# A reordered DeltaNet preparation in a hybrid encoder layer

## The chip, the cores and the metric

The kernel runs on one core of one Trainium2 chip. A core has a matrix engine (TensorE, in the profile PE, with its weight loads as PEld), a vector engine (VectorE, DVE), a scalar engine (ScalarE, ACT), a general engine (GpSimd, POOL) and a queue engine (SyncE, SP) that here issues nearly all transfers. The metric is the device time of one execution in microseconds (us); lower is better.

## The reference, cut to what matters

One encoder layer is applied with the same weights to two sequences, 1024 and 256 tokens of width 1024. The kernel treats them as ten tiles of 128 tokens.

```
h = RMSNorm_pre(x);  p = h @ w_in            # 3088 columns
group A: bidirectional gated DeltaNet, 4 heads of 128
    q, k, v = silu(depthwise conv of 5 taps (p columns))
    q, k normalised to unit length; per head a decay g and a gain beta, per direction
    in chunks: tri = I + strict_lower(beta * k k^T * decay); solve tri against (beta v, beta k exp(cum g))
    a state of 128x128 is carried from chunk to chunk
    o = o_forward + o_backward;  o = RMSNorm(o) * silu(z)
group B: bidirectional attention, 4 query heads, 2 key heads, RMS-normalised q and k, 2-D rotary positions
x = x + RMSNorm(concat(o_A, o_B) @ w_out)
x = x + RMSNorm(relu(RMSNorm(x) @ w_up)^2 @ w_down)
```

All arithmetic that matters is kept to about 32 bits: a factor is split into a high part and a low part (`split`, lines 79 and 80), and a product is three matmuls.

## The kernel before, in words

The kernel is one function, `build`, traced from top to bottom. A planner then fixes the order of the instructions on each engine: what is traced earlier has the higher priority, and a later instruction is put ahead only where the planner expects the earlier one not to be ready. Each engine, and each DMA queue, then works strictly in the fixed order and waits where an input or a buffer is not ready. A buffer is named by a tag with a number of copies; a tile that takes a copy waits until the last reader of the tile before it is done.

The layer goes through these stages:

1. *Normalisation and z* (0 to 96 us). `x_proc` (lines 176 to 185) normalises a token tile (square on ACT, an inverse root in ten small DVE steps, a multiplication on DVE), transposes it on PE and splits it into `h_hi` and `h_lo`. `load_block` loads and splits the weights of the z columns; the low parts are subtracted on POOL (`leng=G`). `nat_z` multiplies, ten tiles in turn. Masks (`incl`, `strict`, `identr`, `nmask`, lines 237 to 246) are traced after that loop, but nothing keeps the planner from putting them first.
2. *Preparation* (96 to 525 us), the loop over `ORDER` at the end of the first half. Its parts are generators, and each word of `ORDER` runs one of them as far as its next `yield`:
   - `K` (`gdn_qk`): for a head, projects k, then its convolution (`conv_proj`), transposes k (L459), writes decayed keys; the same for q (transposes L473); then the inverse lengths.
   - `V` (`gdn_v`): the same for v (transposes L502).
   - `E` (`gdn_e`), five parts of two tiles: decay exponents `pe` by matmuls (L516, L522) with a right side `ER` (L518: one direction on POOL, one on DVE), `E = exp(pe)` (L523), products `pk` of k with k and q (L528), and from both the tiles `A` (L529) and `C` (L531).
   - `S` (`gdn_sub`): inverts the 32x32 diagonal blocks of C, with a chain of 62 DVE instructions per head (L560, L561).
   - `L` (`gdn_lev`): two levels that build the inverse of 128x128 from these blocks, with small matmuls (L589 to L625).
   - `a` (`att_proj`): an attention column block; j = 0 to 3 are queries, 4 and 5 keys, 6 and 7 values. Projects, transposes on PE for the sums of squares (L400), and for queries and keys applies the rotary positions: the rows swapped in groups of 32 are got by writing the block to DRAM (`aqkv_d`, L391) and loading it back swapped (`axw`, L394). Keys are multiplied by a broadcast inverse length, `prk` (L423, L426).
   Every projection (`proj_T`, L367 to L369) is 72 matmuls. They need `h_hi` and `h_lo`, whose space the attention stage takes over afterwards.
3. *Attention with the DeltaNet scan* (525 to about 800 us): the first scores (L712) need the keys and queries loaded from DRAM (`load_rot`, L663); the scan loads what the preparation wrote to `vis_d` (`vis_load`, L652).
4. *Output projection and the feed-forward part*, to the end.

PSUM has eight banks: in the preparation `mm` has three (projections), `tr` two (`pe` and `pk` among others), and `tq` (kt, qt, vt), `iv` (levels) and `at` (attention transposes, `prk`) one each.

Of the kernel before, what the change touches and what calls it, by code (L numbers as in the profile page):

```python
# [38 lines left out]
ORDER = (  # L39
    "K0 K0 K0 K0 E0 E0 E0 E0 K1 E0 K1 S0 K1 K1 L0 E1 E1 V0 V0 E1 E1 L0 E1 K2 K2 K2 K2 E2 E2 E2 V1 E2 E2 "  # L40
    "V1 S1 K3 S2 K3 K3 L1 L1 V2 K3 L2 V2 V3 V3 E3 L2 a0 a0 E3 E3 a4 E3 E3 a4 S3 L3 a5 L3 a5 a6 a6 a1 a1 "
    "a2 a2 a3 a3 a7 a7"
)
# [18 lines left out]
def build(ctx, tc, I, O):  # L62
# [48 lines left out]
    z_d = dr.tile([TOK, 512], F32, name="z_d")  # L111
    aqkv_d = [dr.tile([128, TOK], F32, name=f"aqkv{j}_d") for j in range(6)]
    arot_d = [dr.tile([128, TOK], F32, name=f"arot{j}_d") for j in range(8)]
# [14 lines left out]
    tr_tile = b_tile("tr", 2, ps)  # L128
    tq_tile = b_tile("tq", 1)
    iv_tile = b_tile("iv", 1)  # L130
    at_tile = b_tile("at", 1)
    ch_tile = b_tile("ch", 2)
# [44 lines left out]
    def x_proc(t, x):  # L177
        junk = xs.tile([128, DM], F32, tag="junk", name="junk", bufs=1)
        ss = xs.tile([128, 1], F32, tag="ss", name="ss", bufs=3)
        S.activation(junk, x, AF.Square, accum_out=ss)  # L180
        rs = xs.tile([128, 1], F32, tag="rs", name="rs", bufs=3)
        rsqrt(xs, rs, ss, 1, 1.0 / DM, "n0")
        xn = xs.tile([128, DM], F32, tag="xn", name="xn", bufs=2)
        V.scalar_tensor_tensor(xn, x, rs, wpre, ALU.mult, ALU.mult)
        to_T(xs, xn, h_hi, h_lo, t)


    w_in = I["w_in"]

    def load_block(segs):  # L190
        wts = []
        for k in range(KD):
            raw = xp.tile([128, 512], F32, tag="wraw", name="wraw", bufs=4)
            o = 0
            for c0, n in segs:
                SP.dma_start(out=raw[:, o:o + n], in_=w_in[k * 128:(k + 1) * 128, c0:c0 + n])
                o += n
            whi = xp.tile([128, 512], F32R, tag="whi", name="whi", bufs=8)
            wlo = xp.tile([128, 512], F32R, tag="wlo", name="wlo", bufs=8)
            split(whi, wlo, raw, leng=G)  # L200
            wts.append((whi, wlo))
# [21 lines left out]

    x_proc(0, x)
    wz = load_block([(1536, 512)])

# [3 lines left out]
    for t in range(NT):  # L230
        if t + 1 < NT:
            x_proc(t + 1, x_load(t + 1))
        nat_z(t, wz)
# [9 lines left out]
    identr = gc.tile([128, 128], F32R, name="identr")  # L243
    V.tensor_copy(identr, ident)
    nmask = gc.tile([128, 2, 128], F32R, name="nmask")
    V.tensor_scalar(nmask, f32(strict), -1e30, None, ALU.mult)
    ones1 = gc.tile([128, 1], F32, name="ones1")
# [132 lines left out]
    def att_proj(j):  # L380

        if not att:
            rope = gp.tile([128, 2, 1282], F32, tag="qk", name="rope", bufs=2)[:, :, 0:1024]
            SP.dma_start(out=rope, in_=I["c_rope"])
            att[0] = rope
        rope = att[0]
        c = (2064 + j * 128, 2576 + (j - 4) * 128, 2832 + (j - 6) * 128)[max(0, j - 2) // 2]
        raw = tp_.tile([128, TOK], F32, tag="cp", name="araw", bufs=2)
        proj_T(c, raw, ((0, 512, 0), (512, 512, 512), (1024, 256, 1024)))
        if j < 6:  # L390
            SP.dma_start(out=aqkv_d[j], in_=raw)  # L391
            xw = tp_.tile([128, TOK], F32, tag="cy", name="axw", bufs=1)
            for b in range(4):
                SP.dma_start(out=xw[b * 32:b * 32 + 32], in_=aqkv_d[j][(b ^ 1) * 32:(b ^ 1) * 32 + 32])  # L394
        yield
# [12 lines left out]
        if j >= 6:  # L408
            return
        rs = rsa[:, j]  # L410
        rsqrt(gp, rs, ssa[:, j], NT, 1.0 / 128, "na")
# [38 lines left out]
    def gdn_qk(h):  # L450
        qk = gp.tile([128, 2, 1282], F32, tag="qk", name="qk", bufs=2)
        qks[h] = qk
        yield from conv_proj(4 + h, qk[:, 1])
        ssq = gp.tile([128, 2, NT], F32, tag="ssq", name="ssq", bufs=2)
# [12 lines left out]
        yield  # L467
        yield from conv_proj(h, qk[:, 0])
        for t0 in range(0, NT, 4):
# [24 lines left out]
    def gdn_v(h):  # L494
        vT = gp.tile([128, 1282], F32, tag="vT", name="vT", bufs=1)
        yield from conv_proj(8 + h, vT)
        irk = irks[h]
        for t0 in range(0, NT, 4):
# [9 lines left out]
    def gdn_e(h):  # L508
# [3 lines left out]
        for t0, n in ((0, 2), (2, 2), (4, 2), (6, 2), (8, 2)):  # L512
            E = gp.tile([128, 2, 2, 128], F32, tag="E", name="E", bufs=2)
            pe = tr_tile("pe").rearrange("p (d j c) -> p d j c", d=2, j=2)
            for d in range(2):
                T.matmul(pe[:, d], lhsT=identr, rhs=nmask[:, 1 - d:2 - d].to_broadcast([128, 2, 128]), start=True, stop=False)  # L516
                R = gp.tile([128, 2, 2, 128], F32R, tag="ER", name="ER", bufs=1)
                (G if d == 0 else V).tensor_tensor(  # L518
                    R, incl[:, d][:, None, None, :].to_broadcast([128, 2, 2, 128]),
                    f32(gr[:, :, t0:t0 + 2, 4 * d + h])[:, :, :, None].to_broadcast([128, 2, 2, 128]), ALU.mult)  # L520
                for i in range(2):
                    T.matmul(pe[:, d], lhsT=(r_gt, r_lt)[d], rhs=R[:, i], start=False, stop=(i == 1))  # L522
            S.activation(E, pe, AF.Exp)  # L523
            A = gp.tile([128, 2, 2, 128], F32, tag="A", name="A", bufs=1)
            for j in range(n):
                t = t0 + j
                pk = tr_tile("pk")
                T.matmul(pk[:, 0:256], lhsT=qk[:, 1, col(t)], rhs=qk[:, :, col(t)], start=True, stop=True)  # L528
# [10 lines left out]
    def gdn_sub(h):  # L539
        C = Cs[h]  # L540

        Cc = gp.tile([128, 2, NT, 32], F32, tag="Cc", name="Cc", bufs=1)
        for b in range(4):
# [978 lines left out]
```

## Time and profile before

| | |
|---|---|
| time, median of 3 runs | 1723.78 us (1721.43 to 1723.92) |
| time of the profiled execution | 1724.17 us |
| its span in the profile | 1722.4 us |
| busy share of the span: PE, PEld, DVE, ACT, POOL | 94%, 80%, 74%, 49%, 42% |
| mean granted PE clock | 0.985 |
| data moved by DMA | 252.68 MB |

A row of a table of stretches gives the stretch in us from the start of the span, its length, then for each engine the busy time with the number of instructions, the granted PE clock (1.00 is full), the share in which the DMA engines were busy, and GB/s. A row of waits gives the engine, its tile and line, what released it, the total in us, how many times, and the longest. A row of a group of instructions gives line, engine, operation, output and inputs, shape and count; then busy us and the mean of one in ns; then the idle time just before them and what ended it. A row of a timeline gives start, duration, engine, line and operation, and in square brackets the idle time ahead of it with what ended it. A row of DMA issues gives target and source, queue, count, KB of one and the median us from issue to landing. A row for PE shows modelled ends: consecutive matmuls overlap.

### The profile page before, as it was taken

Reading aid. Unit: us, or ns where it says so; the run is one execution under the profiler, and the core shown is the slowest. Engines: PE = TensorE matmul, PEld = TensorE weight load, DVE = VectorE, ACT = ScalarE, POOL = GpSimd, SP = SyncE. Lnnn points to the kernel's source line nnn. Section 1 sums busy time; section 2 is a strip of 40 time slices with the busy share of each in tenths; the row PEclk is TensorE's granted clock in tenths of the full one; section 3 lists DMA queues with packets and bytes.
Section 4 is the critical chain, followed back from the end, with each engine's and each line's share of the span. In section 5 each row is a group of like instructions: output and inputs, shape, how many; then the busy total and the mean of one; then the engine's idle time right before and its main releaser. Section 6 shows DMA issues by size and latency. Waiting matters only on the chain. (4 is left out here: it accounts for less than half of the span.)

```text
span 1722.4 us, 27988 instructions
## 1 busy us (share of the span) xinstructions
PE 1618.9 (94%) x9799; PEld 1383.8 (80%) x9799; DVE 1278.8 (74%) x2562; ACT 851.8 (49%) x1937; POOL 715.4 (42%) x645
## 2 busy tenths in 40 slices
PE   6999898899997999889998999999999999999996
PEld 5877676777776888668877999999998888888885
DVE  7546798997654788885659759555797887887877
ACT  5226567654345767674436546554464333333412
POOL 3212231312113434440103634644335778878852
PEclk9999999999998999999999999999999999999998
DMA  6213344545547866244334445434566444444244
GB/s 201 79 35 105 103 111 127 147 109 164 150 142 222 289 196 206 80 162 157 110 110 132 159 140 177 149 130 141 191 217 214 144 141 143 141 128 146 82 137 150
DMA packets 208779, 252.68 MB, mean 147 GB/s; under 512 B 35073, under 2 KB 163391, under 8 KB 208639
## 3 DMA queue, kind: packets, MB, share of 16 engines
q1 hardware_dynamic: 208495, 250.77, 46.2%
q8 instruction: 77, 1.26, 0.3%
q14 instruction: 63, 0.52, 0.1%
q0 software_dynamic: 144, 0.13, 0.0%
HBM read 159.75 MB, written 91.10 MB: 146 GB/s over the span
## 5 line engine op out<-in xcount | busy, mean ns | idle before, releaser
L1161 PE MATMUL pd<-mh,uhl 128*128 128x320 f32 x892 | 277.5, 311 | 6.0 <-DVE uhl L1152 5.9
L1160 PE MATMUL pd<-mh,uhl 128*128 128x320 f32 x892 | 276.0, 310 | 1.9 <-ACT uhl L1151 1.9
L1162 PE MATMUL pd<-ml,uhl 128*128 128x320 f32 x892 | 276.2, 310 | 0.0
L1309 DVE TENSOR_TENSOR acc<-acc,pd 128x512 f32<-128x512 f32 x330 | 207.4, 679 | 48.4 <-PE pd L1305 47.9
L1303 PE MATMUL pd<-dhi,fhi 128*128 128x512 f32 x490 | 192.2, 392 | 0.9 <-DVE acc L1311 0.9
L1304 PE MATMUL pd<-dl,fhi 128*128 128x512 f32 x490 | 192.3, 392 | 0.0
L1305 PE MATMUL pd<-dhi,flo 128*128 128x512 f32 x490 | 191.9, 392 | 0.0
L367 PE MATMUL pt<-h_hi,whi 128*128 128x512 f32 (+1 forms) x480 | 177.8, 370 | 0.0
L368 PE MATMUL pt<-h_lo,whi 128*128 128x512 f32 (+1 forms) x480 | 177.7, 370 | 0.0
L369 PE MATMUL pt<-h_hi,wlo 128*128 128x512 f32 (+1 forms) x480 | 177.4, 370 | 0.0
L1161 PEld LDWEIGHTS pd<-mh,uhl 128*128 128x128 f32 x892 | 168.3, 189 | 8.6 <-DVE uhl L1152 8.6
L1160 PEld LDWEIGHTS pd<-mh,uhl 128*128 128x128 f32 x892 | 168.0, 189 | 3.6 <-ACT uhl L1151 3.5
L1162 PEld LDWEIGHTS pd<-ml,uhl 128*128 128x128 f32 x892 | 168.1, 188 | 0.0
L1285 ACT CAST fhi<-fr 128x1280 fp32r<-128x1280 f32 x49 | 62.1, 1267 | 201.1 <-PE pd L1304 114.5
L1206 POOL TENSOR_TENSOR s<-u,u 128x320 f32<-128x320 f32 x31 | 28.2, 909 | 252.9 <-ACT u L1170 252.9
L1275 POOL TENSOR_TENSOR dl<-dw,dhi 128x1024 fp32r<-128x1024 f32 x47 | 118.7, 2525 | 28.3 <-ACT dhi L1274 20.8
L1152 DVE TENSOR_TENSOR uhl<-us,uhl 128x512 fp32r<-128x512 f32 x88 | 90.2, 1025 | 37.5 <-ACT uhl L1151 36.6
L727 POOL TENSOR_TENSOR P<-P,sm 128x512 f32<-128x512 f32 (+1 forms) x72 | 73.5, 1042 | 94.9 <-DVE sm L725 40.0
L1303 PEld LDWEIGHTS pd<-dhi,fhi 128*128 128x128 f32 x490 | 92.0, 188 | 22.2 <-issue 1.3
L1305 PEld LDWEIGHTS pd<-dhi,flo 128*128 128x128 f32 x490 | 92.0, 188 | 20.6
L1304 PEld LDWEIGHTS pd<-dl,fhi 128*128 128x128 f32 x490 | 92.0, 188 | 20.5
L1169 ACT ACTIVATE u<-u 128x320 f32<-128x320 f32 x128 | 60.1, 470 | 95.4 <-DVE u L1196 40.8
(369 smaller groups left out, 4116.4 us busy)
## 6 DMA issues: line engine op xcount, KB each, us to landing
fr<-r_d SPq DMA_DIRECT2D x49, 640.0 KB, 3.9
vis<-vis_d SPq DMA_DIRECT2D x64, 384.0 KB, 4.2
uraw<-in_w_up SPq DMA_DIRECT2D x22, 1024.0 KB, 5.4
r_d<-s SPq DMA_DIRECT2D x128, 160.0 KB, 1.8
r_d<-u SPq DMA_DIRECT2D x96, 160.0 KB, 1.9
dw<-in_w_down SPq DMA_DIRECT2D x28, 512.0 KB, 4.3
wraw<-in_w_in SPq DMA_DIRECT2D x48, 256.0 KB, 3.4
x<-in_x_prompt SPq DMA_DIRECT2D x16, 512.0 KB, 3.5
```

The costliest lines, as they stand in the source:

```text
L367: T.matmul(pm[:, :n], lhsT=whi, rhs=h_hi[:, k, t0:t0 + n], start=(k == 0), stop=False)
L368: T.matmul(pm[:, :n], lhsT=whi, rhs=h_lo[:, k, t0:t0 + n], start=False, stop=False)
L369: T.matmul(pm[:, :n], lhsT=wlo, rhs=h_hi[:, k, t0:t0 + n], start=False, stop=(k == KD - 1))
L1152: V.tensor_tensor(lo, ua[n][UP[i][0]], f32(hi), ALU.subtract)
L1160: T.matmul(pm, lhsT=w[0][:, k], rhs=mh[b, i][:, k], start=(k == 0), stop=False)
L1161: T.matmul(pm, lhsT=w[1][:, k], rhs=mh[b, i][:, k], start=False, stop=False)
L1162: T.matmul(pm, lhsT=w[0][:, k], rhs=ml[b, i][:, k], start=False, stop=(k == 3))
L1275: last["pool"] = leng.tensor_tensor(lo, raw, f32(hi), ALU.subtract)
L1303: T.matmul(pm, lhsT=r[0][:, k, tk], rhs=w[0][:, k], start=(k == 0), stop=False)
L1304: T.matmul(pm, lhsT=r[0][:, k, tk], rhs=w[1][:, k], start=False, stop=False)
L1305: T.matmul(pm, lhsT=r[1][:, k, tk], rhs=w[0][:, k], start=False, stop=(k == Q - 1))
L1309: last["dve"] = V.tensor_tensor(half(t, d), half(t, d), pm, ALU.add)
```

## The change

The parts of the preparation are cut differently, listed in another order, and take other buffers.

- `ORDER` is replaced. The sub-block solves S and the E parts of a head come earlier, the attention projections all come after S3, and L3 comes at the very end.
- `gdn_qk`, `gdn_v` and `att_proj` yield once more, so that the transposes of k, q and v come a part after the convolution, and the tail of an attention block a part after its transposes.
- `tq`, `iv` and `at` become one ring of three PSUM banks, `fx`; `pk` moves from `tr` to that ring. `ER` and `A` get a second copy. `Cc` takes the buffer of `Rt`.
- The ER tile of one direction is made by four ACT instructions where POOL made it with one.
- The swapped rows are copied from `raw` to `axw` inside SBUF; `aqkv_d` is gone. `axw` takes the second `qk` buffer and alternates between its two halves.
- The low parts of the z weights are subtracted on DVE, placed behind the first tile's normalisation in DVE's queue (`issue_after` orders instructions of one engine); `identr` and `nmask` are placed behind the normalisation of the last tile.

```diff
 ORDER = (
-    "K0 K0 K0 K0 E0 E0 E0 E0 K1 E0 K1 S0 K1 K1 L0 E1 E1 V0 V0 E1 E1 L0 E1 K2 K2 K2 K2 E2 E2 E2 V1 E2 E2 "
-    "V1 S1 K3 S2 K3 K3 L1 L1 V2 K3 L2 V2 V3 V3 E3 L2 a0 a0 E3 E3 a4 E3 E3 a4 S3 L3 a5 L3 a5 a6 a6 a1 a1 "
-    "a2 a2 a3 a3 a7 a7"
+    "K0 K0 K0 K1 K0 K0 E0 E0 K1 E0 E0 K1 E0 S0 V0 K1 K1 E1 L0 V0 E1 L0 E1 V0 E1 K2 E1 S1 K2 V1 K2 K2 V1 K2 V1 E2 L1 E2 "
+    "K3 E2 L1 E2 K3 E2 S2 K3 V2 K3 V2 K3 V2 E3 L2 V3 E3 E3 L2 V3 E3 E3 V3 S3 a4 a4 a5 a5 a4 a0 a5 a0 a1 a0 a1 a6 a1 "
+    "a2 a6 a2 a3 a2 a3 a7 a3 L3 a7 L3"
 )
...
-    aqkv_d = [dr.tile([128, TOK], F32, name=f"aqkv{j}_d") for j in range(6)]
...
-    tq_tile = b_tile("tq", 1)
-    iv_tile = b_tile("iv", 1)
-    at_tile = b_tile("at", 1)
+    tq_tile = iv_tile = at_tile = b_tile("fx", 3)
...
-            split(whi, wlo, raw, leng=G)
+            split(whi, wlo, raw)
...
-    x_proc(0, x)
-    wz = load_block([(1536, 512)])
+    done = x_proc(0, x)
+    with tc.issue_after(done.ins):
+        wz = load_block([(1536, 512)])
...
-            x_proc(t + 1, x_load(t + 1))
+            done = x_proc(t + 1, x_load(t + 1))
...
-    V.tensor_copy(identr, ident)
     nmask = gc.tile([128, 2, 128], F32R, name="nmask")
-    V.tensor_scalar(nmask, f32(strict), -1e30, None, ALU.mult)
+    with tc.issue_after(done.ins):
+        V.tensor_copy(identr, ident)
+        V.tensor_scalar(nmask, f32(strict), -1e30, None, ALU.mult)
...
     def att_proj(j):
-        if not att:
+        if not att and j < 6:
             rope = gp.tile([128, 2, 1282], F32, tag="qk", name="rope", bufs=2)[:, :, 0:1024]
             SP.dma_start(out=rope, in_=I["c_rope"])
-            att[0] = rope
-        rope = att[0]
+            att["rope"] = rope
+            att["xw"] = gp.tile([128, 2, 1282], F32, tag="qk", name="axw", bufs=2)
+        rope = att.get("rope")
...
         if j < 6:
-            SP.dma_start(out=aqkv_d[j], in_=raw)
-            xw = tp_.tile([128, TOK], F32, tag="cy", name="axw", bufs=1)
+            xw = att["xw"][:, j % 2, 0:TOK]
             for b in range(4):
-                SP.dma_start(out=xw[b * 32:b * 32 + 32], in_=aqkv_d[j][(b ^ 1) * 32:(b ^ 1) * 32 + 32])
+                SP.dma_start(out=xw[b * 32:b * 32 + 32], in_=raw[(b ^ 1) * 32:(b ^ 1) * 32 + 32])
         yield
...
         if j >= 6:
             return
+        yield
         rs = rsa[:, j]
...
     def gdn_qk(h):
...
-        yield from conv_proj(4 + h, qk[:, 1])
+        pk_, pq_ = conv_proj(4 + h, qk[:, 1]), conv_proj(h, qk[:, 0])
+        next(pk_)
+        yield
+        next(pq_)
+        next(pk_, None)
+        yield
         ssq = gp.tile([128, 2, NT], F32, tag="ssq", name="ssq", bufs=2)
...
         yield
-        yield from conv_proj(h, qk[:, 0])
+        next(pq_, None)
+        yield
...
     def gdn_v(h):
         vT = gp.tile([128, 1282], F32, tag="vT", name="vT", bufs=1)
         yield from conv_proj(8 + h, vT)
+        yield
...
-                R = gp.tile([128, 2, 2, 128], F32R, tag="ER", name="ER", bufs=1)
-                (G if d == 0 else V).tensor_tensor(
-                    R, incl[:, d][:, None, None, :].to_broadcast([128, 2, 2, 128]),
-                    f32(gr[:, :, t0:t0 + 2, 4 * d + h])[:, :, :, None].to_broadcast([128, 2, 2, 128]), ALU.mult)
+                R = gp.tile([128, 2, 2, 128], F32R, tag="ER", name="ER", bufs=2)
+                gd = f32(gr[:, :, t0:t0 + 2, 4 * d + h])
+                if d == 0:
+                    for i in range(2):
+                        for j in range(2):
+                            S.activation(R[:, i, j], incl[:, d], AF.Copy, scale=gd[:, i, j:j + 1])
+                else:
+                    V.tensor_tensor(R, incl[:, d][:, None, None, :].to_broadcast([128, 2, 2, 128]),
+                                    gd[:, :, :, None].to_broadcast([128, 2, 2, 128]), ALU.mult)
...
-            A = gp.tile([128, 2, 2, 128], F32, tag="A", name="A", bufs=1)
+            A = gp.tile([128, 2, 2, 128], F32, tag="A", name="A", bufs=2)
...
-                pk = tr_tile("pk")
+                pk = tq_tile("pk")
...
-        Cc = gp.tile([128, 2, NT, 32], F32, tag="Cc", name="Cc", bufs=1)
+        Cc = gp.tile([128, 2, NT, 32], F32, tag="Rt", name="Cc", bufs=1)
```

More of the change, by code (lines that the diff above doesn't have):

```diff
@@ L183, in x_proc @@
         xn = xs.tile([128, DM], F32, tag="xn", name="xn", bufs=2)
-        V.scalar_tensor_tensor(xn, x, rs, wpre, ALU.mult, ALU.mult)
+        done = V.scalar_tensor_tensor(xn, x, rs, wpre, ALU.mult, ALU.mult)
         to_T(xs, xn, h_hi, h_lo, t)
+        return done
     w_in = I["w_in"]
```

## The prediction, made before the changed kernel ran

> **What bounds the kernel now.** I read the page's engine totals first, then the table of stretches, then the list of what TensorE (PE) waited for in the stage that the change touches, then single moments.
>
> ```profile
> PE 1618.9 (94%) x9799; PEld 1383.8 (80%) x9799; DVE 1278.8 (74%) x2562; ACT 851.8 (49%) x1937; POOL 715.4 (42%) x645
> ```
>
> ```profile
> core 0: us, PE busy (x) PEld busy (x) DVE busy (x) ACT busy (x) POOL busy (x), PEclk, DMA share, GB/s
> ...
> 9.94:37.00 27.06, 22.12 (x86) 16.88 (x86) 22.23 (x50) 14.99 (x28) 12.90 (x11) 0.94 0.60 183
> ...
> 110.00:210.00 100.00, 89.06 (x460) 72.35 (x461) 63.30 (x112) 60.17 (x170) 24.54 (x29) 0.98 0.37 102
> 210.00:430.00 220.00, 200.04 (x1780) 161.47 (x1779) 194.49 (x442) 128.29 (x341) 56.97 (x132) 0.97 0.47 128
> 430.00:525.00 95.00, 88.46 (x713) 70.61 (x711) 55.23 (x160) 35.88 (x124) 17.07 (x36) 0.98 0.49 143
> 525.00:540.00 15.00, 8.08 (x28) 6.14 (x29) 6.37 (x13) 6.07 (x15) 2.47 (x3) 0.66 0.88 285
> ```
>
> PE is busy 94% of the span, so only what keeps PE waiting can be won. The change lies in the first 540 us: the gate columns z (10 to 90 us), the preparation (96 to 525) and its end. From 110 to 430 us PE is busy 289.1 of 320, so it stands still 30.9 us; from 430 to 525 another 6.5. VectorE (DVE) is the second engine to watch: 63% busy from 110 to 210, but 194.49 of 220 (88%) from 210 to 430. Between its small dependent instructions that is close to full.
>
> ```profile
> PE pe L516 <- DVE C L531: 7.1, 6, 2.5
> PE ps_s L712 <- ACT q_hi L79: 6.4, 1, 6.4
> PE vt L502 <- DVE vT L446: 6.1, 3, 2.1
> PE prk L423 <- DVE araw L426: 4.8, 2, 3.4
> PE qt L473 <- DVE qk L446: 3.6, 2, 2.2
> PE pk L528 <- DVE prod L560: 2.2, 1, 2.2
> PE kt L459 <- DVE qk L446: 1.9, 1, 1.9
> ...
> PE pe L522 <- DVE ER L518: 1.4, 1, 1.4
> ...
> PE kt L459 <- issue: 1.2, 1, 1.2
> ```
>
> Columns: total us, times, longest. Three kinds stand here. PE reaches a transpose (vt, qt, kt) while DVE is still on the last step of the convolution: 6.1 + 3.6 + 1.9 + 1.2 = 12.8 us. PE cannot open the next decay tile (pe), or multiply into it, because the two PSUM banks that pe and pk share, or the one ER buffer, are still read: 7.1 + 2.2 + 1.4 = 10.7. And prk has a single bank: 4.8. A long stall costs more than itself, because the clock drops behind it:
>
> ```profile
> 158.00:161.30 3.30, 1.26 (x6) 0.69 (x4) 2.99 (x16) 1.27 (x1) 0.59 (x4) 1.00 0.00 0
> 161.30:164.00 2.70, 2.64 (x9) 2.30 (x10) 2.43 (x4) 0.00 (x0) 0.00 (x0) 0.57 0.00 0
> 164.00:167.00 3.00, 2.94 (x19) 2.55 (x18) 0.09 (x1) 1.94 (x8) 0.98 (x1) 0.81 0.68 218
> ```
>
> After a stall of about 2 us the granted clock is 0.57 and then 0.81. Lost: 2.70 x 0.43 + 3.00 x 0.19 = 1.7 us.
>
> **The change part by part.** The sum is made against the profiled execution, 1724.17 us (span 1722.4 and 1.8 around it), 0.4 above the median of 1723.78.
>
> *First tiles.* The masks leave the head of DVE's queue, and the eight subtractions of z's low parts go from POOL to DVE.
>
> ```profile
> 5.34 0.19 ACT L180 ACTIVATION_READ_ACCUMULATOR junk<-x 128x1 f32 x1
> ...
> 6.29 0.29 DVE L246 TENSOR_SCALAR nmask<-strict 128x256 fp32r<-128x256 f32 x1 [6.29 <-DMA strict<-in_c_cst]
> ...
> 6.63 0.15 DVE L88 TENSOR_SCALAR n0x<-ss 128x1 f32<-128x1 f32 x1
> ...
> 13.98 5.01 POOL L80 TENSOR_TENSOR wlo<-wraw,whi 128x512 fp32r<-128x512 f32 x4
> ...
> 15.31 1.22 DVE L98 SCALAR_TENSOR_TENSOR n0y<-n0t,n0y 128x1 f32<-128x1 f32 x1
> ...
> 19.04 0.22 DVE L94 SCALAR_TENSOR_TENSOR n0t<-n0y,n0h 128x1 f32<-128x1 f32 x1
> ...
> 21.96 1.94 PE L171 MATMUL xt<-ident,xn 128*128 128x128 f32 x8 [3.41 <-DVE n0x L88]
> ```
>
> The sum of squares is there at 5.53 (5.34 + 0.19), yet DVE first waits for the strict mask and starts tile 0 at 6.63: up to 1.1 us at the very head. Then, while POOL subtracts (13.98 to 18.99), single-element DVE steps take 1.22 us in place of 0.22; five such steps between 13.9 and 20.5 make tile 1 late and PE stands 3.41 us, then runs slow. The eight subtractions cost DVE some 0.69 to 0.83 us each (row below), 5.5 to 6.7, about what the stretched steps cost it now (five times 1.0); PE's feed of z weights arrives sooner, since a raw buffer is released after 0.7 us and not 1.4. Ends: -1.1 - 3.4 - 1.5 (slow clock) = -6 if all goes, 0 if DVE, 22.23 of 27.06 busy here, takes the stall's place. I take -4, nearer to the first end because the work on DVE stays the same and POOL's interference ends.
>
> *Transposes one part later.* No instruction is added; kt, qt and vt, now up to 12.8 us of PE waits, come behind another projection. One projection is long enough to hide a convolution's tail:
>
> ```profile
> 113.17 0.40 PE L367 MATMUL pt<-h_hi,whi 128*128 128x512 f32 x1
> ...
> 129.47 0.39 PE L367 MATMUL pt<-h_hi,whi 128*128 128x512 f32 x1
> ```
>
> From the first matmul of one to the first of the next are 16 us, with little between them. *Ring of three banks, two ER and two A buffers.* pk no longer sits in pe's banks, so 10.7 us lose their cause, and prk gets three banks for its three tiles: 4.8 us. The price is that pk now shares with the transposes (the rival below).
>
> *R on ACT.* Twenty POOL instructions become eighty of 128x128 on ACT.
>
> ```profile
> L518 POOL TENSOR_TENSOR ER<-incl,gr 128x512 fp32r<-128x512 f32 x20 | 28.6, 1429 | 69.7 <-PE pe L522 69.7
> ...
> L464 ACT ACTIVATE kn<-kt,cum 128x128 f32<-128x128 f32 x80 | 22.6, 397 | 0.3 <-DMA vis_d<-kn 0.2
> ```
>
> ```profile
> L80 DVE TENSOR_TENSOR wlo<-wraw,whi 128x512 fp32r<-128x512 f32 x37 | 30.8, 833 | 19.4 <-ACT whi L79 16.9 <-DMA vis_d<-A 2.5
> ```
>
> By the nearest row, kn, R takes 4 x 0.40 = 1.6 us against 1.43: 32 us more for ACT, which is 128.29 of 220 busy in the dense stretch. Behind PE's other work that is nothing; with the cover gone it is 20 x 0.16 = 3 us. In return DVE is held up less: its wlo step averages 833 ns here, 0.69 where nothing disturbs it. I enter 0, bounds -5 and +3.
>
> *The new order.* The same instructions, but the sub-block solves and the E parts start earlier, where DVE had 36.7 us idle (110 to 210), and the attention projections, which need little DVE, all come after them. The named stalls from 110 to 430 are 12.8 + 10.7 = 23.5 us and three clock dips (161, 209, 264 us), 5 us. Every one of them ends with DVE, and DVE at 88% can hand back a stall that a buffer hid. So I take half: -14; ends 0 and -28. From 430 to 525 prk's wait and the dip behind it, 4.8 + 1.7, mostly go: -5, ends 0 and -6.5. That a solve's Cc now takes Rt's buffer, and so waits until the level work of the head before it has left it, is inside these ends.
>
> *Swapped rows inside SBUF.* Six writes of 640 KB go; 24 loads stay.
>
> ```profile
> aqkv_d<-araw SPq DMA_DIRECT2D x6, 640.0 KB
> axw<-aqkv_d SPq DMA_DIRECT2D x24, 160.0 KB, 3.5
> ...
> SPq L394 <- DMA aqkv_d<-araw: 6.2, 3, 3.4
> SPq L573 <- DMA r_d<-Rm: 4.8, 3, 2.3
> ...
> SPq L630 <- ACT C L628: 6.8, 2, 5.1
> ```
>
> Every DMA is issued by one in-order queue (SP); it stood 6.2 us for the round trip, and the weights of the next projection are queued behind. PE's list shows no wait for weights, so 0, bounds -4 (one DVE wait of 3.7 for axw that prk then passes on) and +3 (the first load needs a qk buffer that head 3 must leave; a4's projection hides it).
>
> *Last levels last.* The end is a hole: after the last projection the attention's k and q are loaded, and PE idles 6.4 us, then runs at 0.66. Head 3's level matmuls now come there:
>
> ```profile
> L618 PE MATMUL ph<-X,C 64*64 64x64 f32 x160 | 6.4, 223 | 1.2 <-ACT H L620 1.2
> L625 PE MATMUL py<-C,H 64*64 64x64 f32 x160 | 6.4, 223 | 0.0
> ```
>
> A quarter of these two is 3.2 us, and the smaller level about as much again, so some 6 us of PE work can fill the hole. Ends: -7, and +8 where the attention's loads are queued in SP behind the levels' own chain (r_d to Rc up to 2.3, the final C up to 5.1). I take -5.
>
> Sum: -4 - 14 - 5 - 5 = -28; 1724.2 - 28 = **1696 us**.
>
> [...]
>
> **The rivals.**
>
> *DVE hands the stalls back.* All preparation stalls end with DVE; if it is the true bound of 210 to 430 us, removing PSUM reasons only renames them. For it: 88%. Against: DVE's 36.7 idle us before 210, which the order reaches. Then first tiles (-4), prk with its dip (-5) and a third of the end (-2) remain: 1713.
>
> *All named stalls go.* -6, -28, -6.5, -7: -47.5, so 1677. For it: each wait has its edit. Against: in-order engines seldom lose every wait at once.
>
> *The shared ring turns against PE (slower).* kt, qt and vt had a bank nobody else used; now a pk bank is held until DVE has done one A (0.41) and two C (0.34 each), 1.1 us, and 36 transpose tiles (twelve groups of three) may stand behind it. 36 x 1.1 = 40 us, against the 28 won: +12, 1736. It decides from 28/36 = 0.8 us per tile. For it: pk's readers queue behind solves on DVE. Against: three banks, and today's PE waits have C as releaser only six times.
>
> ```profile
> L529 DVE TENSOR_TENSOR A<-E,pk 128x256 f32<-128x256 f32 x40 | 16.5, 412 | 10.6 <-ACT E L523 7.3 <-PE pk L528 1.6 <-DMA vis_d<-A 1.6
> L531 DVE SCALAR_TENSOR_TENSOR C<-pk,sca,E 128x128 f32<-128x128 f32 x80 | 24.3, 341 | 0.4 <-DMA vis_d<-C 0.4
> ```
>
> *It does not do what it says.* The instructions' order on each engine is fixed by a planner before the run; if it had already reordered around the listed parts, the new list changes little: 1722.
>
> **How the numbers follow.** Forecast 0.55, its own range 1683 to 1708; DVE hands back 0.20; all go 0.08; nothing changes 0.07; ring 0.10. The range takes in the forecast, the first two rivals and the bounds: 1672 to 1719, leaving out about 0.17. Within 0.2% (3.4 us) is what a measurement of this kernel cannot tell from no change. Faster by more: 0.55 + 0.20 + 0.08 = 0.83; same 0.07; slower 0.10.
>
> **What would show it.** Right: the first PE instruction near 9 us and no 3 us gap before 25; the lines vt, qt, kt, pe<-C and prk<-araw gone or under 1 us each; granted clock 1.00 in nearly all stretches from 110 to 430; the last projection ending near 500; first attention scores within a few us of it, with level matmuls in between; DVE busier before 210. Wrong: the same waits under other names with DVE as releaser (first rival), waits of kt, qt or vt on C or A (ring), attention scores waiting behind vis or C writes (the end).

## The result: 66 us slower

| | median | range |
|---|---|---|
| before | 1723.85 us | 1721.43 to 1729.17 |
| changed | 1790.22 us | 1788.84 to 1792.96 |

The ratio is 1.0376, with a 95% interval of 1.0353 to 1.0398. The prediction was 1696 us, in a range of 1672 to 1719, so it had the wrong sign. The changed kernel's profiled execution has a span of 1787.8 us (before: 1722.4). Of the further kernels below, one execution of `own_cc` (2063.18 us) and one of `small_edits` (2644.02 us) ran at a granted clock of 0.74 and 0.56; the ratios leave these two out.

**The profile after.** First the page's totals of the changed kernel and its table of stretches, with the cuts that the prediction used.

```profile
PE 1630.3 (91%) x9799; PEld 1400.7 (78%) x9799; DVE 1276.3 (71%) x2570; ACT 870.7 (49%) x2017; POOL 675.4 (38%) x617
```

```profile
core 0: us, PE busy (x) PEld busy (x) DVE busy (x) ACT busy (x) POOL busy (x), PEclk, DMA share, GB/s
9.36:37.00 27.64, 25.17 (x111) 18.57 (x112) 26.01 (x73) 18.05 (x34) 3.40 (x3) 1.00 0.72 225
110.00:210.00 100.00, 94.77 (x506) 79.51 (x505) 71.81 (x132) 74.65 (x217) 15.33 (x29) 0.98 0.37 102
210.00:430.00 220.00, 173.61 (x1351) 141.04 (x1349) 153.05 (x334) 108.57 (x294) 33.90 (x104) 0.89 0.36 97
430.00:525.00 95.00, 57.47 (x511) 46.90 (x512) 65.50 (x189) 32.59 (x121) 13.81 (x41) 0.71 0.39 106
```

Up to 210 us the change does what was forecast: PE starts at 9.36 (before 9.94), and from 110 to 210 it stands still 5.2 us where it stood 10.9. Then it turns over. From 210 to 430 PE is idle 46.4 us (before 20.0), from 430 to 525 it is idle 37.5 (before 6.5), and the granted clock falls to 0.89 and 0.71. DVE did not become busier, as a DVE bound would have it: 153.05 of 220 after 194.49. PE and DVE are both idle more, so they wait for each other. The list of PE's waits up to 640 us names the places.

```profile
PE ph L602 <- DVE Rt L589: 26.7, 2, 22.2
PE prk L424 <- DVE araw L427: 14.9, 1, 14.9
PE qt L480 <- ACT kn L470: 11.9, 4, 6.1
...
PE pe L535 <- ACT ER L530: 4.6, 5, 1.8
...
PE pe L535 <- DVE ER L532: 2.1, 1, 2.1
...
PE pk L541 <- DVE C L544: 1.9, 1, 1.9
...
PE kt L465 <- DVE C L544: 1.0, 3, 0.6
```

Most waits for which the change was forecast to pay are indeed gone: of pe on C (7.1) and pk on DVE (2.2) there is 1.9 left, and kt, qt and vt no longer wait for the convolution. The wait of `pe` for ER, which a second buffer was to end, grew from 1.4 to 6.7 us. Others take their place: 22.2 us in front of a level's first product `ph`, 14.9 us in front of `prk`, and `qt` now waits 11.9 us for ACT, which still reads `kt` (into `kn`) out of the bank that `qt` is to get.

Where the 65.4 us of span stand is read from two groups, the attention scores and the scan's first products, before and after (the times behind the comma are the first and the last start).

```profile
L712 PE MATMUL ps_s<-k_hi,q_hi x72: 278/474/796, 531.3 to 765.8; 128*128 128x512 f32 x64, 128*128 128x256 f32 x8
L810 PE MATMUL p<-vis x32: 275/275/421, 535.8 to 559.2; 128*128 128x128 f32 x32
```

```profile
L725 PE MATMUL ps_s<-k_hi,q_hi x72: 281/476/795, 586.1 to 830.1; 128*128 128x512 f32 x64, 128*128 128x256 f32 x8
L823 PE MATMUL p<-vis x32: 273/275/497, 595.6 to 616.0; 128*128 128x128 f32 x32
```

The preparation ends 54.8 us later (531.3 to 586.1), the scan starts 59.8 later, and the last scores come 64.3 later. So 55 us are lost in the preparation and about 10 in the attention stage.

**The 22 us in detail.** First a row of the view of one tile, `vT` (the last two times before the shape are its first and last start), then rows of the changed kernel's timeline:

```profile
L447 DVE SCALAR_TENSOR_TENSOR vT<-vT,cy x1: 1496/1496/1496, 403.7 to 403.7; 128x1282 f32<-128x1282 f32 x1
```

```profile
413.63 0.60 ACT L536 ACTIVATE E<-pe 128x512 f32<-128x512 f32 x1 [7.41 <-DVE C L544]
418.16 0.28 PE L369 MATMUL pt<-h_hi,wlo 128*128 128x256 f32 x1
432.99 0.34 SPq L582 DMA_DIRECT2D r_d<-Rm  x1
439.75 0.84 DVE L589 STREAM_TRANSPOSE Rt<-Rc 128x640 f32<-128x640 f32 x1 [0.44 <-DMA Rc<-r_d]
440.65 0.26 PE L602 MATMUL ph<-Rt,C 32*32 32x32 f32 x2 [22.21 <-DVE Rt L589]
445.50 3.78 PE L541 MATMUL pk<-qk 128*128 128x256 f32 x8
455.02 0.64 PE L510 MATMUL vt<-ident,vT 128*128 128x128 f32 x4 [0.16 <-DVE C L544]
```

Head 3's `E` is there at 385.1 for its second part and at 414.2 for its third, and its convolved `vT` at 405.2. The next `pk` and `vt` have everything they need, but `pk` is multiplied at 445.50 and `vt` transposed at 455.02. They stand behind `ph`, the first tile of L2, which waits for the solve S2 on DVE and two DMA hops (433 to 439.75). All of them turn in the one ring `fx`, and a ring gives its banks out in the order in which the tiles were traced: `ph` has its turn before it has its data, and `py` and `px` of the same level have the next two of the three turns. The order of PE's matmuls that the planner made shows the same (tile and how many in a row; `pt` are projections, `ph` to `px` levels):

```
before:  vt4 pt3 ph40 pt2 vt2 py40 pt8 px20 ... at3 pt6 ph40 at4 pt1 py40 pt1 at2 ... prk4 pt14 ph40 pt3 py40 pe4 pk1
changed: pe6 pt259 ph40 pt3 py40 px20 pk1 ... pe6 pt226 ph40 py40 px20 pk4 ... pe6 pt25 ph40 py40 px20 pk4 ... pk4 vt10 at20 prk20
```

Before, projections are strewn between the small tiles. Changed, 259 and 226 projection matmuls in a row stand ahead of the first two levels, and ahead of the third only 25. The other parts of E3, which the last solve needs, then come late, and S3 on DVE in turn holds up the attention's keys (`prk`, 14.9 us).

The projections do not run out: these 25 end the third attention block, five more are to come, and yet the next projection matmul starts at 492.9, 74.7 us after the last (before, no such break is longer than 6 us). Rows of ACT and SP in the changed kernel, then one of SP in `level_bank`, where the levels have a bank of their own (see below):

```profile
399.31 1.35 ACT L370 COPY araw<-pt 128x512 f32<-128x512 f32 x3
...
492.27 1.35 ACT L370 COPY araw<-pt 128x512 f32<-128x512 f32 x3 [23.00 <-DVE axw L417]
```

```profile
463.20 0.61 SPq L394 DMA_DIRECT2D axw<-araw  x1
```

```profile
400.71 0.61 SPq L395 DMA_DIRECT2D axw<-araw  x1
```

The first two attention blocks are complete at 343 and 401 us and fill both buffers of `araw`. The third is multiplied by 418.4, but can't be copied out of the three `mm` banks until 492.27. The tail of the first block waits for its transposes `at`, which have their turn in the ring at 457.2, and for its swapped rows, whose buffer `axw` is head 3's `qk`: the last `pk` that reads it starts at 454.5, and the rows go from 463.20 on (in `level_bank` 400.04 and 400.71). So what holds E3 also holds the tail, the blocks and, through them, the projections that could have covered the wait. How much the rows' buffer adds in this kernel was not measured.

### The profile page after: what moved, and what is told of

It is laid out like the page before. It is cut to its first block, busy times and chain, and to the rows that moved or that the text cites. A ratio compares the mean times of both kernels' runs of the same rounds, so it can differ in the third digit from the quotient of the medians.

```text
span 1787.8 us, 28047 instructions
## 1 busy us (share of the span) xinstructions
PE 1630.3 (91%) x9799; PEld 1400.7 (78%) x9799; DVE 1276.3 (71%) x2570; ACT 870.7 (49%) x2017; POOL 675.4 (38%) x617
## 5 line engine op out<-in xcount | busy, mean ns | idle before, releaser
L369 PE MATMUL pt<-h_hi,wlo 128*128 128x512 f32 (+1 forms) x480 | 173.6, 363 | 6.6 <-DVE wlo L80 6.6
L369 PEld LDWEIGHTS pt<-h_hi,wlo 128*128 128x128 f32 x480 | 91.4, 190 | 22.1 <-DVE wlo L80 8.1
```

The costliest lines, as they stand in the source:

```text
L369: T.matmul(pm[:, :n], lhsT=wlo, rhs=h_hi[:, k, t0:t0 + n], start=False, stop=(k == KD - 1))
```

## The experiments

Each ratio is against runs of the kernel before on the same chip, with its 95% interval.

| kernel | median us | ratio |
|---|---|---|
| ring_only | 1816.07 | 1.0506 (1.0489 to 1.0523) |
| level_bank | 1750.69 | 1.0144 (1.0111 to 1.0178) |
| old_rings | 1767.10 | 1.0231 (1.0196 to 1.0265) |
| order_only | 1755.07 | 1.0147 (1.0122 to 1.0172) |
| old_order | 1795.57 | 1.0401 (1.0367 to 1.0435) |
| small_edits | 1755.91 | 1.0153 (1.0135 to 1.0171) |
| first_only | 1720.63 | 0.9947 (0.9927 to 0.9966) |
| own_cc | 1790.40 | 1.0366 (1.0332 to 1.0400) |
| r_act_only | 1761.41 | 1.0204 (1.0170 to 1.0238) |
| er2_only | 1752.65 | 1.0150 (1.0130 to 1.0171) |
| pool_r | 1792.48 | 1.0387 (1.0366 to 1.0408) |
| axw_only | 1750.42 | 1.0146 (1.0111 to 1.0182) |
| cc_only | 1741.69 | 1.0097 (1.0061 to 1.0134) |
| tqat2 | 1726.80 | 0.9999 (0.9980 to 1.0018) |
| pk_pair | 1742.81 | 1.0101 (1.0080 to 1.0122) |
| fixed | 1761.12 | 1.0199 (1.0173 to 1.0225) |
| fixed_pair | 1753.21 | 1.0156 (1.0132 to 1.0180) |
| pair_vals | 1745.01 | 1.0104 (1.0087 to 1.0122) |

### The ring

`ring_only` is the kernel before with the ring, `level_bank` the changed kernel with a bank of its own for the levels, `old_rings` the changed kernel with the banks of before and `pk` back in `tr`.

```diff
 ring_only (on before)
-    tq_tile = b_tile("tq", 1)
-    iv_tile = b_tile("iv", 1)
-    at_tile = b_tile("at", 1)
+    tq_tile = iv_tile = at_tile = b_tile("fx", 3)
-                pk = tr_tile("pk")
+                pk = tq_tile("pk")
 level_bank (on changed)
-    tq_tile = iv_tile = at_tile = b_tile("fx", 3)
+    tq_tile = at_tile = b_tile("fx", 2)
+    iv_tile = b_tile("iv", 1)
```

> The kernel before with nothing but the PSUM ring: tq, iv and at become one ring of three banks and pk moves into it. Ring theory (a level tile waiting for its solve holds its turn, and what is traced behind it cannot pass): this alone makes the kernel slower by 30 to 75 us, 1755 to 1800, with ph waiting for Rt. If the ring hurts only under the new list: 1710 to 1730.

> The changed kernel, but of the ring of three banks one goes back to the levels alone (two banks stay for kt, qt, vt, pk, at and prk). Ring theory (a level tile that waits for its solve holds its turn in the shared ring, so pk, kt, qt, vt and at traced behind it cannot pass): the waits of ph for Rt (26.7 us) and most of the low-clock time go, 1715 to 1745 us. Order theory (the new list puts each level too close behind its solve, whatever the banks): PE waits for Rt again, 1775 to 1795. Buffer theory (Cc in Rt's buffer chains solve to level to solve): 1775 to 1795.

> The changed kernel with the PSUM tiles of before: tq, iv and at one bank each, pk in tr. Ring theory: as the run with the levels' own bank or better, 1700 to 1735 us, and the waits of pe for C come back (several us). Order theory and buffer theory: 1775 to 1795.

PE's wait in front of a level in `ring_only`, then in `level_bank`, then the costliest wait of `old_rings`:

```profile
PE ph L587 <- DVE Rt L574: 55.4, 3, 26.5
```

```profile
PE ph L603 <- DVE Rt L590: 3.6, 1, 3.6
```

```profile
PE prk L426 <- DVE araw L429: 25.8, 4, 20.0
```

Alone, the ring costs 87 us, more than the whole change, and PE waits 55.4 us, three times, in front of a level. In the changed kernel a bank for the levels brings that wait from 26.7 down to 3.6 us and gives back 40 of the 66 us. With the banks of before, 25 come back and another wait appears, `prk` behind DVE: its 20.0 us end at 428.98, while DVE works at S2 (from 403.7 on). The ring theory had the direction right and the sizes wrong: `ring_only` is slower than its 1755 to 1800, and the other two stay above their 1715 to 1745 and 1700 to 1735. So the ring holds most of the loss, through the levels' turn in it, and not all of it.

### The list, and the late solves

`order_only` is the kernel before with the new list and cuts; `old_order` the changed kernel with the list and cuts of before.

> The kernel before with nothing but the new list and the new cuts (the extra yields). Ring theory as the whole cause: 1690 to 1722 us, the gain that was predicted of the order. Second cause in the order (solve 3 runs on DVE ahead of the tails of the first attention blocks, and the levels of head 3 stand alone at the end): 1735 to 1770, with PE waiting 10 us or more in prk and about 20 us of level work behind the last projection.

> The changed kernel with the list and the cuts of before; ring, ER, A, R on ACT, swapped rows in SBUF, Cc in Rt and the first tiles stay changed. Order theory: 1700 to 1725 us. Ring theory: the ring blocks under this list too, 1750 to 1800, with ph waiting for Rt.

A wait of PE in `order_only`; then, from SP's timeline of `order_only` and of the kernel before, the last writes of C and the first loads of the scan.

```profile
PE prk L424 <- DVE araw L427: 10.2, 3, 8.5
```

```profile
546.04 0.52 SPq L638 DMA_DIRECT2D vis_d<-C  x1
...
553.15 33.02 SPq L660 DMA_DIRECT2D vis<-vis_d  x36
```

```profile
507.34 0.53 SPq L629 DMA_DIRECT2D vis_d<-C  x1
...
529.42 2.74 SPq L652 DMA_DIRECT2D vis<-vis_d  x6
```

The list alone costs 26 us by the median. Its scores start at 540.8, 9.5 later than before; most of that is `prk` behind the solve S3. The rest is at the end: with L3 last, the scan's loads are issued at 553.15 in place of 529.42, 24 us later, and the spans differ by 24.8. So what was to fill a hole of 6 us moved the start of the scan. That this also moves the end is read from these times; no run puts L3 alone at the end. In `old_order` the list of before does not help, since the ring holds its parts too (27.6 us of `ph` for Rt, in three waits).

Three more kernels asked whether the list pays once nothing holds its parts. `fixed` is the changed kernel with a ring of two beside a bank for the levels, R on POOL and Cc in its own buffer (A then has one copy); `fixed_pair` is that with the banks of before and both `pk` of a part in one tile of `tr`; `pair_vals` is `fixed_pair` with the value blocks, which have no tail on DVE, directly behind S3.

```diff
 fixed (on changed)
-    tq_tile = iv_tile = at_tile = b_tile("fx", 3)
+    tq_tile = at_tile = b_tile("fx", 2)
+    iv_tile = b_tile("iv", 1)
-        Cc = gp.tile([128, 2, NT, 32], F32, tag="Rt", name="Cc", bufs=1)
+        Cc = gp.tile([128, 2, NT, 32], F32, tag="Cc", name="Cc", bufs=1)
 pair_vals (on fixed_pair), the end of the list
-E3 V3 S3 a4 a4 a5 a5 a4 a0 a5 a0 a1 a0 a1 a6 a1 a2 a6 a2 a3 a2 a3 a7 a3 L3 a7 L3
+E3 V3 S3 a6 a6 a7 a7 a4 a4 a5 a5 a4 a0 a5 a0 a1 a0 a1 a2 a1 a2 a3 a2 a3 L3 a3 L3
```

> The changed kernel with three of its edits undone or mended: the levels have a bank of their own beside a ring of two, R is on GpSimd again, Cc has its own buffer (A one copy for the room). The list, the cuts, the first tiles, two ER and the rows in SBUF stay. If the list is good once nothing holds its parts (theory blocked gain), it beats the first-tile edits alone: 0.985 to 0.995 of before. If the list has a loss of its own (theory list, 26 us alone on the kernel before, less 9 of the first tiles), it is 1.004 to 1.015.

> The changed kernel with the banks of before (one each for transposes, levels and attention), the paired pk tile in the two banks of pe, R on GpSimd and Cc in its own buffer; the list, the cuts, the first tiles, two ER and the rows in SBUF stay. Theory blocked gain: 0.985 to 0.995 of before. Theory list: 1.004 to 1.015, and against the kernel with the ring of two it shows whether any shared bank is worth having: less than 5 us apart if not.

> The changed kernel with the banks of before, the paired pk, R on GpSimd and Cc in its own buffer (1.0156 of before, with 17.6 us in which TensorE waits for Rt of L2 while VectorE works at the last solve), and in the list the two value blocks a6 and a7, which have no tail on VectorE, directly behind S3. If the list's loss is that nothing covers the last solve (theory cover), the wait of 17.6 us goes below 5 and the time falls by 10 to 25 us: 1.001 to 1.010 of before. If the loss lies elsewhere (theory spread), the wait moves to another tile behind VectorE and it stays within 1.012 to 1.02.

The costliest wait of `fixed`, of `fixed_pair` and of `pair_vals`:

```profile
PE prk L425 <- DVE araw L428: 25.3, 2, 23.1
```

```profile
PE ph L600 <- DVE Rt L587: 17.7, 2, 17.6
```

```profile
PE prk L426 <- DVE araw L429: 6.5, 4, 3.4
```

All three lose, so the list does not pay with the ring, R and Cc undone or mended. `fixed` and `fixed_pair` lie even above the 1.004 to 1.015 of theory list. The three do not show what the list costs by itself, as `order_only` does, since the two ER and the rows inside SBUF stay in them. PE stands at a tile that needs DVE while DVE solves, and which tile that is depends on the banks: in `fixed_pair` it is `ph` of L2, which waits for S2 (its DVE steps start between 381.1 and 413.1, the wait ends at 421.05), not for the last solve, as I had put it. With two blocks behind S3 that need little of DVE, that wait is gone, and the kernel gains about 9 us (1.0156 to 1.0104), a little less than the 10 to 25 expected. The longest break between projection matmuls fits: 57.1, 45.1 and 23.2 us in the three kernels. `pair_vals` reaches its first scores at 535.2, 3.9 later than before, and yet its span is 21.7 longer. Its scan starts at 544.1, 8.3 later, and its last product of `p` comes at 744.7, 20.2 later; that the scan starts behind L3 is seen, why it also takes longer is open.

### The small edits

`small_edits` is the changed kernel with the list, cuts and banks of before; `first_only` the kernel before with the first tiles' edits alone; `own_cc` the changed kernel with a buffer for Cc (and one A).

> The changed kernel with list, cuts and PSUM banks of before: what stays are the first tiles, R on ACT, second copies of ER and A, the swapped rows inside SBUF, and Cc in Rt's buffer. If ring and order are the whole loss: 1700 to 1722 us. If one of the edits that stay costs (Cc in Rt, R on ACT): 1735 to 1760.

> The kernel before with nothing but the edits of the first tiles (masks behind the normalisations, z low parts on DVE). In the trace of the changed kernel the preparation begins 4.8 us earlier (first projection matmul at 90.9 us, before 95.7), so 1717 to 1721 us if that reaches the end, 1722 to 1726 if it does not.

> The changed kernel with Cc in a buffer of its own, as before; to make room A has one copy again. Buffer theory: the chain solve, level, solve opens and the time falls to 1720 to 1750 us. Ring theory and order theory: within 10 us of the changed kernel, 1780 to 1800.

The first tiles' edits gain 8.8 us by the median, while the others together cost some 35, which I had not expected of any. Each was then made alone on the kernel before: R on ACT with two ER (`r_act_only`), two ER with R on POOL (`er2_only`), the rows inside SBUF (`axw_only`), Cc in the buffer of Rt (`cc_only`). `pool_r` is the changed kernel with R on POOL.

```diff
 er2_only (on before)
-                R = gp.tile([128, 2, 2, 128], F32R, tag="ER", name="ER", bufs=1)
+                R = gp.tile([128, 2, 2, 128], F32R, tag="ER", name="ER", bufs=2)
 cc_only (on before)
-        Cc = gp.tile([128, 2, NT, 32], F32, tag="Cc", name="Cc", bufs=1)
+        Cc = gp.tile([128, 2, NT, 32], F32, tag="Rt", name="Cc", bufs=1)
 axw_only (on before)
+            att["xw"] = gp.tile([128, 2, 1282], F32, tag="qk", name="axw", bufs=2)
...
-            SP.dma_start(out=aqkv_d[j], in_=raw)
```

> The kernel before with the E parts' first R as four ScalarE activations in place of one GpSimd multiply, and two ER buffers; nothing else. The kernel with all small edits stood some 35 us above the one with the first tiles' edits alone, so one of three edits carries most of it. If R on ScalarE does (theory R: 80 more activations on an engine whose E, kn and cp copies the chain of parts needs, and another planned order), this kernel is 20 to 35 us slower than before. If the rows or Cc do, it is within 6 us of before.

> The kernel before with two ER buffers, both R still on GpSimd and VectorE; nothing else. R on ScalarE with two ER buffers cost 35 us alone. If ScalarE's queue is what costs (theory ScalarE), this one is within 6 us of before. If the second ER buffer, which lets a part's pe run ahead of its pk, is (theory run ahead), it is 20 to 35 us slower.

> The changed kernel with the first R made by one GpSimd multiply again; all else as changed. Alone on the kernel before, the R edit cost 35 us. If costs add (theory sum), this kernel is 25 to 40 us faster than the changed one: 1.014 to 1.024 of before. If the ring's turns set the end in the changed kernel and ScalarE's part is hidden behind them (theory overlap), it is within 10 us of the changed one: 1.032 to 1.044.

> The kernel before with the attention's swapped rows copied inside SBUF, into a buffer of the qk ring; nothing else. Theory X: under the list of before, a0 starts while the last head's E part still reads its qk, so the swapped rows' buffer comes free only behind E3; a0's exchange and everything behind it on its buffers wait: 15 to 35 us slower, with a wait of SyncE or VectorE on E3's last products. If the exchange itself is all there is (theory 0), it is within 5 us of before, rather below, since ten DMAs' way through DRAM is gone.

> The kernel before with Cc in the buffer of Rt; nothing else. Theory C: a solve can't begin before the level part ahead of it has read Rt for the last time; in the list of before S1 and S2 stand ahead of L1, so the next head's solve is held, and the levels behind it: 8 to 25 us slower. Theory 0: the levels ahead are over anyway, within 4 us of before, as the own buffer made no difference in the changed kernel.

*Rows inside SBUF.* A row of SP's timeline of `axw_only`, and what ACT and PE waited for (ACT from 380 to 450 us):

```profile
422.26 4.16 SPq L393 DMA_DIRECT2D axw<-araw  x4
```

```profile
ACT araw L369 <- DMA arot_d<-araw: 14.1, 1, 14.1
```

```profile
PE pt L366 <- ACT araw L369: 17.1, 2, 15.7
```

The first swapped rows go at 422.26, behind the last `pk` of head 3 (419.5), because `axw` takes head 3's qk buffer; before, their first loads went at 374.54. a0's block stays in its buffer so long that PE's projections stop for 15.7 us. *Cc.* The fourfold copy into Cc of head 1 starts at 239.51 before and at 289.15 here, after L0 has read Rt (transposed at 281.80): the solve starts 50 us later, behind the level ahead of it, and `cc_only` loses 15. Both expectations named these mechanisms. In the changed kernel the list has S1 behind L0, and `own_cc`, which also gives up the second A, makes no difference. It has all attention blocks behind E3 too, but the planner puts three of them ahead, so there the rows wait for head 3's last `pk` as well (463.20, above).

*R and ER.* The second ER buffer alone costs 26 of the 35 us. With it the planner puts all six matmuls of `pe` together. Its first scores come at 555.9, 24.6 later than before, so the loss lies in the preparation. No single wait in the trace of `er2_only` accounts for it; the list shows many of 2 to 3 us, and how the loss comes about is open. R on ACT adds some 9 us (1.0150 to 1.0204, on different chips). From the groups and from DVE's waits of `r_act_only`:

```profile
L522 ACT ACTIVATE ER<-incl,gr 128x128 fp32r<-128x128 f32 x80 | 28.6, 414 | 9.6 <-PE pe L527 9.5
```

```profile
DVE wlo L80 <- ACT whi L79: 37.0, 14, 7.8
```

The eighty instructions take 414 ns each, as estimated (0.40), and DVE waits 37.0 us for ACT's halves of the weights; before it was 16.9 (in `er2_only` 26.6). In the changed kernel R on POOL changes nothing beyond the error, in the range of theory overlap. But this undoes only the part that costs some 9 us alone, since the two ER stay.

### Were the waits worth anything?

`tqat2` takes the first tiles' edits and one ring of two banks for kt, qt, vt, at and prk; `pk_pair` takes them and one tile for the two `pk` of a part, so that `pe` no longer waits for C.

```diff
 tqat2 (on first_only)
-    tq_tile = b_tile("tq", 1)
-    at_tile = b_tile("at", 1)
+    tq_tile = at_tile = b_tile("tq", 2)
 pk_pair (on first_only)
-                pk = tr_tile("pk")
+            pk2 = tr_tile("pk")          # ahead of the loop over j
+                pk = pk2[:, 256 * j:256 * j + 256]
```

> The kernel before with the first tiles' edits, and the bank of kt, qt, vt and the bank of at, prk made one ring of two; the levels keep their own bank. If a ring is only bad where a level's tile stands in it (theory H), the waits of kt, qt and vt for their one bank go (12.8 us in the profile before) without new ones: 5 to 15 us below the first-tile edits alone, 0.985 to 0.992 of before. If any shared ring brings head-of-line waits (theory A: prk waiting for the rotation holds up vt and kt behind it), it is 1.00 to 1.02 of before.

> The kernel before with the first tiles' edits and one tile pk for the two tokens' products of an E part in place of two, in the same two banks; nothing else. Now pe and pk take turns, one bank each, and pe of the next part no longer waits for the C products of this one. If those waits (7.1 us in the profile before) are on the path: 5 to 10 us below the first-tile edits alone, 0.988 to 0.993 of before. If they are filled by projections or come back as pk waiting for C: 0.993 to 0.998.

The costliest PE wait of the preparation in `tqat2`, then in `pk_pair`:

```profile
PE vt L504 <- DVE vT L448: 8.5, 3, 3.0
```

```profile
PE pk L532 <- DVE C L535: 10.8, 7, 4.7
```

Neither gains. In `tqat2`, `vt` waits for the same DVE step as it did, 8.5 us in place of 6.1, and the 8.8 us of the first tiles are lost again; a stall that DVE hands back is the first rival's case, but these 2.4 us are not the whole loss. In `pk_pair`, outside both of its ranges, the wait for C moves from `pe` to `pk` and grows from 7.1 to 10.8 us; the kernel is 16 us slower than before and some 26 slower than `first_only`, most of which this wait does not explain. Its longest such wait, in the timelines of DVE and PE:

```profile
228.57 0.34 DVE L535 SCALAR_TENSOR_TENSOR C<-pk,sca,E 128x128 f32<-128x128 f32 x1
```

```profile
228.96 1.22 PE L532 MATMUL pk<-qk 128*128 128x256 f32 x2 [4.74 <-DVE C L535]
```

The second token's product starts at 228.96, where the first token's last C ends (228.91), and the row names that C as what ended 4.74 us in which PE stood idle: here PE wrote one half of the tile only when DVE had read the other. So the pairing replaced one wait by another, and what `pe`'s wait alone is worth stays open.

## Why the prediction was wrong

- **First tiles, -4: the start came as forecast, its way to the end is open.** The projections begin at 90.9 where they began at 95.7, so -4.8 in the changed kernel. Made alone, the edits gain 8.8 us by the medians (0.3 to 0.7% of the time). In `first_only` the wait of 3.41 us is gone, and the single-element steps between 13.9 and 20.5 us, five of which took some 1.2 us, take at most 0.22 in the changed kernel, which has the same edits. But in the profiled execution of `first_only` the first scores come at 531.3, as in the one of before, so the trace does not show where the 8.8 us arise; masks and subtractions were not tried apart.
- **Ring, "10.7 us lose their cause, and prk gets three banks": this step failed.** It counted only what leaves `tr`, and of the three kinds of tile that were thrown together it looked at their number of banks. It did not ask in which order they get them. A level's tile takes its turn 22 us before it has its data, and `pk` and `vt` behind it wait with it. Alone: +87.
- **The ring as a rival was named with the wrong mechanism.** It priced `pk` holding a bank until DVE has read it, 1.1 us for each of 36 transposes. In the trace `qt` does not wait for C, and `kt` and `vt` hardly (1.0 and 0.4 us); `pk` and `vt` wait for `ph`, `ph` for a solve, and `qt` for ACT's reads of `kt`. The price was +12 and the place wrong, so its chance of 0.10 says little.
- **New order, -14 and -5: wrong sign.** Alone it costs 26. I took half of the named stalls without following what is left to cover the solves S2 and S3. Behind S3 the list has only parts that need DVE, and the projections that the planner puts ahead stop when two blocks fill `araw` and a third the `mm` banks: for 74.7 us in the changed kernel, for 30.3 in `order_only`.
- **Transposes one part later: as forecast up to 210 us.** The waits of kt, qt and vt for the convolution are gone from the list, and PE's idle time from 110 to 210 falls by 5.7 us. That PE lacks these projections later, at the solves, fits the order above, but no run shows it alone.
- **Last levels last, -5 (bounds -7 and +8): probably the wrong sign.** I looked at what stands in front of the scores. The scan needs L3's C, and its loads went 24 us later in `order_only`, where the scores came 9.5 later and the end 24.8. The edit was not made alone.
- **R on ACT and the rows in SBUF at 0, Cc inside other ends.** The duration of R was right (0.414 for 0.40). The buffers were not: alone on the kernel before, two ER cost 26, the rows 24, Cc 15. In the changed kernel R on ACT and Cc cost nothing that can be measured; the rows and the two ER were not undone there. For the rows the bound of +3 named the right wait, the qk buffer that head 3 must leave, and took it as hidden by a4's projection: in the changed kernel the first block is complete at 343 us, and its rows go at 463.20.
- **Sum.** Alone, the edits make -9, +87, +26, +35, +24 and +15, together +178, where the change makes +66: costs of this kind do not add, as `pool_r` and `own_cc` show for R on ACT (9 us alone) and Cc (15 us alone), which cost nothing measurable in the changed kernel. I take it that several causes pay for the same idle time of PE. The two A buffers were not tried alone.
- **The signs that would show it wrong** were kept too narrow: the new waits are on `ph` and `prk`, which I had listed under gains or not at all.

**The clock.** The stall of 22 us costs more than itself. Stretches of the changed kernel around it:

```profile
418.40:440.70 22.30, 0.09 (x5) 0.05 (x8) 14.88 (x42) 1.56 (x4) 1.85 (x18) 0.60 0.24 53
440.70:445.00 4.30, 3.13 (x187) 2.86 (x189) 1.68 (x6) 2.40 (x6) 0.00 (x0) 0.50 0.01 4
445.00:450.00 5.00, 5.00 (x43) 3.73 (x41) 4.22 (x14) 1.17 (x3) 0.00 (x0) 0.50 0.19 54
450.00:455.00 5.00, 4.65 (x80) 3.36 (x77) 2.17 (x8) 2.95 (x7) 0.00 (x0) 0.98 0.29 84
```

PE works again from 440.65, but the granted clock stays at 0.50 until about 450. By these rows that is up to half of some 8 busy us, 4 us. The clock was 0.50 through the level's small products with gaps (3.13 busy of 4.30) and through the 5.00 of 5.00 behind them, and 0.98 in the stretch after that.

**A version that beats both** is `first_only`: 1720.63 us, 0.9947 of before (0.9927 to 0.9966), measured on one chip, where all of its executions were below all of before.

## What to carry to other kernels

Before tiles are put into one ring, follow each in the order in which it was traced: a tile that waits for a long chain of another engine holds its turn, and once it and its followers have taken every bank (here three), everything traced behind them waits too (PE stood 22.2 us at `ph` in the changed kernel, and 55.4 us in three such waits in `ring_only`). Where the cover is a stock of independent work (here the projections), ask at each long wait how much of it is left and whether its results have buffers to go to, and move a part to the end only after looking at who needs its output first. In a kernel whose stalls are each 2 to 3 us, an edit that removes one by name can cost ten times as much through the order that the planner then makes (here a second ER: 26 us, for a wait of 1.4), so try each edit alone.

## What I had not expected

A second buffer, with no instruction added or taken away, made the kernel 1.5% slower (`er2_only`, 1752.65 us), and freeing `pe` from its wait for C cost 16 us against the kernel before (`pk_pair`). And `Cc` in the buffer of `Rt` loses 15 us on the kernel before and nothing that can be measured in the changed one, where S1 stands behind L0.
